# Low parts of the weights in the heads' stages: ScalarE's negative and an accumulating transfer in place of VectorE's subtraction

## The chip, the cores and the metric

One Trainium2 chip; the kernel runs on one of its cores. The metric is the device time of one execution in microseconds (us), the median of the runs shown. The engines are TensorE (PE), VectorE (DVE), ScalarE (ACT), GpSimd (POOL) and SyncE (SP), which only issues transfers here. HBM is the memory off the core; tiles live on the core in SBUF, and matmuls end in PSUM.

## The reference, cut to what matters

Two layers over 256 latent tokens, with 256 context tokens ahead of them in the attention and in the scan; the width is 1024, everything is float32.

```python
def layer(x, c):                             # adaLN: shift, scale, gate from c
    h = modulate(rmsnorm(x), shift, scale)
    p = h @ w_in                             # q, k, v, gMLP u and v, HGRN2 gates/q/v, merge gates
    y_att = diff_attention(q, k, v, lam)     # 8 heads: softmax(q1 k1) - lam softmax(q2 k2), times v
    y_gm  = spatial_gating(u, v)             # layernorm(v), a matmul over chunks of 128 tokens, times u
    y_hg  = both_directions(hgrn2_scan)      # 8 heads, keys of 128, values of 128, decays from log f
    y = sig(g0) * (y_att @ wa) + sig(g1) * (y_gm @ wg) + sig(g2) * (y_hg @ wh)
    x = x + gate * rmsnorm(y @ w_out)
    return x + gate2 * conv_ffn(modulate(rmsnorm(x), shift2, scale2))
```

Each weight is used in one projection and is read from HBM as the stage that needs it comes up.

## The kernel before, in words

TensorE multiplies in a form of float32 that keeps fewer bits of an operand (F32R). So each operand is held as two parts, a high part that is the rounded value, and a low part that is what the rounding left, and a product is three matmuls: high by low, high by high, low by high (`mm3`, L120 to L123; its matmuls are the lines L121 to L123).

The parts of a weight are made by `load_part` (L105 to L113), one chunk at a time. A chunk is 128x1024 float32, 512 KB. SP loads it into a tile `wr` (three buffers, L110); ACT casts it to `wh` (four buffers, L111); DVE subtracts, `wl = wr - wh` (four buffers, L112). A tile `wr` is free when cast and subtraction have read it; a `wh` or `wl` when the last matmul has read it.

A layer has a stage of heads (loop at L989 to L1002). In it the matmuls of two things alternate on PE, woven by `weave` (L819): on one side the projections of the next head, which use the weights (`project(h + 1)`: names in_w_hff, in_w_hqg, in_w_aqk, in_w_hi, in_w_av), and on the other side the two halves of head `h`, `hg_head` (the scan, with tiles E, K, w, sqs, sc; L505, L319, L541, L544) and `att_head` (the attention, with tiles p, s, wt; L600 scores, L617 transposes, L624 values). The work of those two between their matmuls is done by DVE, ACT and POOL. Beside the last head stands `tail_proj` (L647) in place of a projection: the weight in_w_gv in two halves of four chunks each, so that one half fills all four buffers of `wl`, and then the first part of in_w_gu in two chunks. PE's order of instructions is fixed by the code as it is written; the order on DVE, ACT and POOL is chosen by the scheduler, which places the loading, cast and subtraction of a weight as early as buffers allow. Each engine works its instructions in order, so that one which waits holds what is behind it.

Layer 0's stage of heads lies at 107 to 648 us of the profiled execution, its `tail_proj` from 562 us on; layer 1's at 1455 to 1862 us, its `tail_proj` from 1800 us on. In each of these stretches lie 64 chunks that the change touches: 42 of in_w_hff, in_w_hqg and in_w_aqk, 12 of in_w_hi and in_w_av, 8 of in_w_gv, 2 of in_w_gu.

Of the kernel before, what the change touches and what calls it, by code (L numbers as in the profile page):

```python
# [10 lines left out]
F32 = mybir.dt.float32  # L11
# [36 lines left out]
def trunk(ctx: ExitStack, tc: tile.TileContext, A, out):  # L48
    nc = tc.nc
    sub, mul, add, amin, amax = ALU.subtract, ALU.mult, ALU.add, ALU.min, ALU.max  # L50
# [9 lines left out]
    @contextmanager  # L60
    def pool(name, side="left", **tags):
        with tc.tile_pool(name=name, bufs=1, side=side, reuse_waits="tile") as p:
            def get(tag, shape, dt=F32):
                return p.tile(shape, dt, tag=tag, name=tag, bufs=tags[tag])
            yield get
# [36 lines left out]
        return pack[l][:, a:b]  # L102


    def load_part(src, k0, k1, eng):  # L105
        w = src.shape[-1]
        raw = wp.tile([P, 1024 // w, w], F32, tag="wr", name="wr", bufs=3)[:, :k1 - k0, :]
        hi = wp.tile([P, 1024 // w, w], F32R, tag="wh", name="wh", bufs=4)[:, :k1 - k0, :]
        lo = wp.tile([P, 1024 // w, w], F32R, tag="wl", name="wl", bufs=4)[:, :k1 - k0, :]
        nc.sync.dma_start(out=raw, in_=src[:, k0:k1, :])  # L110
        nc.scalar.copy(out=hi, in_=raw)  # L111
        eng.tensor_tensor(out=lo, in0=raw, in1=hi.bitcast(F32), op=sub)  # L112
        return [(hi[:, i, :], lo[:, i, :]) for i in range(k1 - k0)]  # L113

    def load_w(src, kt=8, early=True, engs=(nc.vector, nc.vector)):
# [249 lines left out]
    def hg_proj(get, l, h, X, NQ, out, pss=None):  # L365
        ls = get("lk", [P, 2, NT])
        k = get("lk", [P, 2, NT])
        qg = get("qg", [P, 2, NQ])

        def gate(d, ps):  # L370
            t = softplus_neg_abs(get, ps, NT)
            nc.vector.scalar_tensor_tensor(out=k[:, d, :], in0=ps, scalar=0.0, in1=t, op0=amax, op1=add)
            nc.vector.scalar_tensor_tensor(out=ls[:, d, :], in0=ps, scalar=0.0, in1=t, op0=amin, op1=sub)

        if pss is None:
            w = load_w(A["w_hff"][l, h])
            for d in range(2):
                ps = PB([P, 512])
                yield from fm_steps(w, d, X, NT, ps)
                gate(d, ps)  # L380
            w = load_w(A["w_hqg"][l, h])
            for j in range(2):
                ps = PB([P, 512])
                yield from fm_steps(w, j, X, NQ, ps)
                silu_of(get, qg[:, j, :], ps[:, :NQ], NQ)
        else:
            e = get("E", [P, 2, NQ])
            nc.scalar.copy(out=e[:, 0, :], in_=pss[0][:, :NQ])
            nc.vector.tensor_copy(out=e[:, 1, :], in_=pss[1][:, :NQ])
            for d in range(2):  # L390
                gate(d, pss[2 + d])
            for j in range(2):
                silu_of(get, qg[:, j, :], e[:, j, :], NQ)
        out.update(ls=ls, k=k, qg=qg)

    def v_proj(get, src, X, out, name, w=None):
        if w is None:
            w = load_w(src)
        v = get("v", [P, 4, 256])
        for tt in range(2):  # L400
            ps = PB([P, 2, 256])
            yield from tm_steps(w, X, (2 * tt, 2 * tt + 1), ps)
            nc.scalar.copy(out=v[:, 2 * tt:2 * tt + 2, :], in_=ps)
        out[name] = v
# [414 lines left out]
    def weave(main, n, sides, counts, rate):  # L819

        todo = sorted((((i + 1) / (c + 1) * n * rate, k) for k, c in enumerate(counts) for i in range(c)))
        done = 0
        end = object()
        while True:
            while todo and (todo[0][0] <= done or main is None):
                next(sides[todo.pop(0)[1]], None)
            if main is None:
                break
            if next(main, end) is end:
                main = None  # L830
            done += 1
        for g in sides:
            for _ in g:
                pass
# [4 lines left out]
    with pool("x0", side="right", x=4, n=4, h=4, wa=3, wb=3, scr=1, cr=1, wj=1) as get, \  # L839
# [65 lines left out]
        for i in range(KT + 1):  # L905
# [8 lines left out]
            if i:  # L914
                k = i - 1
                for g, ps in enumerate(first):
                    c = slice((g % 2) * P, (g % 2 + 1) * P)
                    hi, lo = w[g // 2][k]
# [16 lines left out]
    for l in range(DEPTH):  # L935
# [5 lines left out]
        def putter(b, h):  # L941
            return lambda t: nc.sync.dma_start(out=ysp[b, h], in_=t)
# [23 lines left out]
        with pool("heads", lk=2, qg=1, qk=1, v=3, w=2, sq=2, sqs=2 if l else 1, wt=2, sc=1, E=6 if l else 4, K=2, p=2) as get, ExitStack() as even, \  # L966
                tc.issue_after(pre.ins):
            gete = even.enter_context(pool("even", lk=2, qg=1, qk=1, t=3, sh=2))
            gets = [lambda tag, *a: (gete if tag in ("lk", "qg", "qk", "t", "sh") else get)(tag, *a),
                    lambda tag, *a: (gete if tag in ("t", "sh") else get)(tag, *a)]  # L970

            def project(h, out, pss=None):
                if pss is not None:
                    yield from hg_proj(gets[h % 2], l, h, Xh, NQ, out, pss)
                if h % 2 == 0:
                    yield from v_proj(get, A["w_hi"][l, h // 2], Xh, out, "vh", whi if h == 0 else None)
                if pss is None:
                    yield from hg_proj(gets[h % 2], l, h, Xh, NQ, out)
                yield from att_proj(gets[h % 2], l, h, Xh, rope, NQ, out)
                if h % 2 == 0:  # L980
                    yield from v_proj(get, A["w_av"][l, h // 2], Xh, out, "va")

            def units(h):
                return (12 if l == 0 else 9) + (8 if h % 2 == 0 else 0)

            d = {}
            for _ in project(0, d, first):
                pass
            for h in range(HEADS):  # L989
                j = slice((h % 2) * P, (h % 2 + 1) * P)  # L990
                m = [hg_head(get, l, h, d["ls"], d["k"], d["qg"][:, 0, :], d["qg"][:, 1, :], d["vh"][:, :, j], putter(1, h),
                             lbv, (reset, masks), NQ),
                     att_head(get, l, d["qk"], d["va"][:, :, j], putter(0, h), attv[l], NQ)]
                if h + 1 < HEADS:
                    main, n = project(h + 1, d), units(h + 1)
                else:
                    even.close()
                    getv = rvt.enter_context(pool("vt", side="right", vt=ns))
                    vt = [getv("vt", [P, D]) for _ in range(ns)]
                    pus = []  # L1000
                    main, n = tail_proj(l, Xh, vt, ns, NQ, pus), 8 * ns // 2 + ns
                weave(main, n, m, (13, 2 * ns + 3), 0.92 if h + 1 < HEADS else (0.7, 0.85)[l])  # L1002
        if l == 0:
            jobs += [(lambda get, scr, m=m: ada_row(get, scr, 0, m, 2)) for m in range(16, 48)]
        pre = nc.scalar.preload_act_table(AF.Gelu_apprx_tanh)
# [204 lines left out]
```

## Time and profile before

| | |
|---|---|
| median of 3 runs | 2241.21 us (2240.69 to 2246.49) |
| profiled execution, its own time | 2245.93 us |
| span of the profile | 2244.2 us |
| PE busy | 2128.5 us, 95% of the span |
| DVE busy | 1727.2 us, 77% |
| ACT busy | 1155.8 us, 52% |
| POOL busy | 324.7 us, 14% |
| queue of SP's transfers | 93042 packets, 290.59 MB |

The busy time of an engine is the time in which it had an instruction at work. An instruction's idle time is the time for which its engine stood still just before it, and the releaser is the work whose end let it go on. The granted clock of TensorE is given as a share of its full speed of 2.4 GHz. A transfer's landing is counted from its issue.

### The profile page before, as it was taken

To read this page: it belongs to the slowest core of one execution; us is meant where nothing else is said; L and a number is where in the kernel's file an instruction comes from. 1 tells how busy PE (TensorE), PEld (TensorE's weight loads), DVE (VectorE), ACT (ScalarE), POOL (GpSimd) and SP (SyncE) were. 2 spreads that over 40 slices of the span, in tenths; PEclk is the share of its full clock that TensorE was granted. 3 is DMA by queue.
4 is the path that set the end of the run, shared out by engine and by line. 5 is a ranking of instruction groups with operands and counts; after the bars stand their busy time and mean duration, and the time that the engine had idled before them with its cause. 6 is when DMAs were issued, how large, how long until landed. Compare 5 with 4: busy or idle time off the path is not lost. (4 is left out here: it accounts for less than half of the span.)

```text
span 2244.2 us, 32759 instructions
## 1 busy us (share of the span) xinstructions
PE 2128.5 (95%) x12400; PEld 1849.0 (82%) x12400; DVE 1727.2 (77%) x2885; ACT 1155.8 (52%) x1913; POOL 324.7 (14%) x276
## 2 busy tenths in 40 slices
PE   6999999999999999998999998999999989997998
PEld 4878888788888877877887877988888879997997
DVE  7799897998857884448876776898998976567786
ACT  3666565665553222335442333666666655456664
POOL 4332132321300000002000001222221210001000
PEclk9999999999999999999999999999999999999999
DMA  7222222122245665344555653222232336554554
GB/s 257 101 71 71 76 76 66 66 71 71 66 149 185 224 201 94 100 141 154 161 179 184 195 144 127 99 91 89 84 96 81 98 98 211 196 192 141 185 195 138
DMA packets 93488, 293.21 MB, mean 131 GB/s; under 512 B 16017, under 2 KB 20753, under 8 KB 93073
## 3 DMA queue, kind: packets, MB, share of 16 engines
q1 hardware_dynamic: 93042, 290.59, 39.9%
q8 instruction: 98, 1.61, 0.3%
q14 instruction: 60, 0.49, 0.1%
q10 hardware_dynamic: 288, 0.52, 0.1%
HBM read 282.66 MB, written 8.41 MB: 130 GB/s over the span
## 5 line engine op out<-in xcount | busy, mean ns | idle before, releaser
L121 PE MATMUL pm<-X,wh 128*128 128x512 f32 (+1 forms) x2032 | 715.8, 352 | 18.2 <-POOL X L253 9.8
L123 PE MATMUL pm<-X,wl 128*128 128x512 f32 (+1 forms) x2032 | 699.0, 344 | 1.2 <-POOL wl L112 1.2
L122 PE MATMUL pm<-X,wh 128*128 128x512 f32 (+1 forms) x2032 | 698.8, 344 | 0.0
L112 DVE TENSOR_TENSOR wl<-wr,wh 128x1024 fp32r<-128x1024 f32 x398 | 492.9, 1243 | 192.6 <-ACT wh L111 187.8
L111 ACT CAST wh<-wr 128x1024 fp32r<-128x1024 f32 x408 | 422.2, 1039 | 313.0 <-PE pm L122 188.3
L121 PEld LDWEIGHTS pm<-X,wh 128*128 128x128 f32 x2032 | 386.5, 190 | 69.1 <-POOL X L253 11.9
L123 PEld LDWEIGHTS pm<-X,wl 128*128 128x128 f32 x2032 | 386.6, 190 | 49.8 <-POOL wl L112 2.7
L122 PEld LDWEIGHTS pm<-X,wh 128*128 128x128 f32 x2032 | 386.3, 190 | 42.1
L225 DVE SCALAR_TENSOR_TENSOR wj<-wa,scr 128x1024 f32<-128x1024 f32 x128 | 156.3, 1221 | 63.8 <-DMA wa<-in_ada_row 60.9
L445 POOL TENSOR_TENSOR K<-qg,E 128x512 f32<-128x512 f32 (+1 forms) x96 | 130.6, 1362 | 466.6 <-PE ps L505 313.6
L121 PE MATMUL pm<-wl,X 128*128 128x256 f32 (+1 forms) x608 | 187.3, 308 | 0.0
L123 PE MATMUL pm<-wh,X 128*128 128x256 f32 (+1 forms) x608 | 183.4, 302 | 0.0
L122 PE MATMUL pm<-wh,X 128*128 128x256 f32 (+1 forms) x608 | 183.2, 301 | 0.0
L202 POOL TENSOR_TENSOR s<-s,mhalf 128x1 f32<-128x1 f32 x26 | 14.4, 552 | 1077.1 <-DVE s L199 1037.1
L121 PE MATMUL pm<-ys,wh 128*128 128x512 f32 (+1 forms) x384 | 129.8, 338 | 8.8 <-ACT wh L111 5.1
L439 DVE TENSOR_TENSOR E<-lk 128x512 f32<-128x512 f32 (+1 forms) x192 | 124.3, 680 | 9.5 <-PE ps L544 8.2
L123 PE MATMUL pm<-ys,wl 128*128 128x512 f32 (+1 forms) x384 | 129.6, 338 | 0.0
L122 PE MATMUL pm<-ys,wh 128*128 128x512 f32 (+1 forms) x384 | 129.4, 337 | 0.0
L121 PEld LDWEIGHTS pm<-wl,X 128*128 128x128 f32 x608 | 117.0, 192 | 6.4 <-issue 2.2
L122 PEld LDWEIGHTS pm<-wh,X 128*128 128x128 f32 x608 | 116.8, 192 | 4.2
L123 PEld LDWEIGHTS pm<-wh,X 128*128 128x128 f32 x608 | 116.6, 192 | 4.3
L440 ACT ACTIVATE E<-E 128x1024 f32<-128x1024 f32 (+1 forms) x96 | 80.8, 846 | 62.7 <-DVE E L439 61.5
(247 smaller groups left out, 3551.8 us busy)
## 6 DMA issues: line engine op xcount, KB each, us to landing
wr<-in_w_up SPq DMA_DIRECT2D x88, 512.0 KB, 4.3
wa<-in_ada_row SPq DMA_DIRECT2D x80, 512.0 KB, 4.1
wr<-in_w_gate SPq DMA_DIRECT2D x48, 512.0 KB, 4.2
wr<-in_w_dn SPq DMA_DIRECT2D x40, 512.0 KB, 4.2
wr<-in_w_hqg SPq DMA_DIRECT2D x32, 512.0 KB, 3.7
wr<-in_w_hff SPq DMA_DIRECT2D x32, 512.0 KB, 3.6
wr<-in_w_aqk SPq DMA_DIRECT2D x32, 512.0 KB, 3.6
wr<-in_w_hi SPq DMA_DIRECT2D x16, 512.0 KB, 4.2
```

The costliest lines, as they stand in the source:

```text
L111: nc.scalar.copy(out=hi, in_=raw)
L112: eng.tensor_tensor(out=lo, in0=raw, in1=hi.bitcast(F32), op=sub)
L121: nc.tensor.matmul(ps, lhsT=lh, rhs=rl, start=first, stop=False)
L122: nc.tensor.matmul(ps, lhsT=lh, rhs=rh, start=False, stop=False)
L123: nc.tensor.matmul(ps, lhsT=ll, rhs=rh, start=False, stop=last)
L202: nc.gpsimd.tensor_tensor(out=r, in0=r, in1=mhalf, op=ALU.pow)
L225: nc.vector.scalar_tensor_tensor(out=junk, in0=raw, scalar=1.0, in1=scr[:, v, :], op0=mul, op1=mul, accum_out=mod[l][:, m, v:v + 1])
L439: nc.vector.tensor_tensor(out=dst, in0=ref if first else src, in1=src if first else ref, op=sub)
L440: nc.scalar.activation(out=E, in_=E, func=AF.Exp)
L445: nc.gpsimd.tensor_tensor(out=mkap(KQ[:], dims, NQ), in0=mkap(q, dims), in1=mkap(E[:], [[2 * b, np_], [b - NQ, 2], [1, b]], NQ), op=mul)
```

## The change

A flag `lean` is set from behind `project(0)` to the end of the loop over the heads, in both layers. While it is set, DVE makes no low part. ACT writes the negative of the high part into `wl`, and a transfer that POOL issues reads the same chunk from HBM once more and adds it to what stands in `wl`. The sum is again `wr - wh`. Outside the flag nothing changes.

```diff
+    lean = [False]
+
     def load_part(src, k0, k1, eng):
...
         nc.sync.dma_start(out=raw, in_=src[:, k0:k1, :])
         nc.scalar.copy(out=hi, in_=raw)
-        eng.tensor_tensor(out=lo, in0=raw, in1=hi.bitcast(F32), op=sub)
+        if lean[0]:
+            nc.scalar.mul(out=lo, in_=hi.bitcast(F32), mul=-1.0)
+            nc.gpsimd.dma_start(out=lo, in_=src[:, k0:k1, :], accum_op=add)
+        else:
+            eng.tensor_tensor(out=lo, in0=raw, in1=hi.bitcast(F32), op=sub)
...
             for _ in project(0, d, first):
                 pass
+            lean[0] = True
             for h in range(HEADS):
...
                 weave(main, n, m, (13, 2 * ns + 3), 0.92 if h + 1 < HEADS else (0.7, 0.85)[l])
+        lean[0] = False
```

Over the whole program DVE has 128 subtractions fewer, ACT 128 instructions more, POOL issues 128 transfers, and 67 MB more are read. PE's order is the same. In the rows below the lines of the changed kernel stand 2 higher up to the cast (L113), and 6 higher behind `load_part` (L612 is L606 of before); L115 is ACT's negative, L116 the accumulating transfer.

The first place is DVE in layer 0, behind the attention's reciprocal of an odd head, where the trace of before has its clearest gap. Before (`wl` is the low part, `sc` the scores of the scan, K and E its keys and exponentials, p and s2 the attention's weights and their scales):

```order
L112 TENSOR_TENSOR wl_2613<-wr_2611,wh_2612 128x1024
L608 RECIPROCAL s2_2299<-s2_2299 128x2
L463 COPY_PREDICATED sc_2253<-masks_541,ps_2343 128x2x2x128
L609 TENSOR_TENSOR s2_2299<-s2_2299,attv_574 128x1
L443 TENSOR_TENSOR K_2372<-lk_1652,E_2368 128x512
L610 TENSOR_SCALAR p_2297<-p_2297,s2_2299 128x512
L439 TENSOR_TENSOR E_2534<-lk_1651 128x256x2
L611 SCALAR_TENSOR_TENSOR p_2297<-p_2297,s2_2299 128x512
L112 TENSOR_TENSOR wl_2619<-wr_2617,wh_2618 128x1024
L463 COPY_PREDICATED sc_2253<-masks_541,ps_2383 128x2x2x128
```

With the change the same place reads as follows (p_2315 and sc_2271 are p_2297 and sc_2253 of before):

```order
L469 COPY_PREDICATED sc_2271<-masks_541,ps_2361 128x2x2x128
L449 TENSOR_TENSOR K_2390<-lk_1660,E_2386 128x512
L445 TENSOR_TENSOR E_2554<-lk_1659 128x256x2
L614 RECIPROCAL s2_2317<-s2_2317 128x2
L445 TENSOR_TENSOR E_2554<-lk_1659 128x256x2
L615 TENSOR_TENSOR s2_2317<-s2_2317,attv_574 128x1
L428 SCALAR_TENSOR_TENSOR lk_2232<-reset_539,lk_2232 128x512
L616 TENSOR_SCALAR p_2315<-p_2315,s2_2317 128x512
L477 COPY s8_2564<-E_2561 128x4
L469 COPY_PREDICATED sc_2271<-masks_541,ps_2401 128x2x2x128
```

The two subtractions between the two copies into `sc` are gone; an instruction for E, the scan and a small copy stand there now.

The second place is ACT beside the last head of layer 0, in `tail_proj`: the casts of the second half of in_w_gv. Before (`vt` takes the projection's result, p and wt are the attention's):

```order
L606 ACTIVATE p,s_5499<-ps,s_5498 128x256 x2
L653 COPY vt<-pm 128x512
L619 COPY wt<-ps 128x512
L111 CAST wh<-wr 128x1024 x4
L653 COPY vt<-pm 128x512
L606 ACTIVATE p,s_5587<-ps,s_5586 128x256 x2
```

With the change:

```order
L612 ACTIVATE p,s_5557<-ps,s_5556 128x256 x2
L659 COPY vt<-pm 128x512
L625 COPY wt<-ps 128x512
L113 CAST wh<-wr 128x1024
L115 ACTIVATE wl<-wh 128x1024
L113 CAST wh<-wr 128x1024
L115 ACTIVATE wl<-wh 128x1024
L113 CAST wh<-wr 128x1024
L612 ACTIVATE p,s_5645<-ps,s_5644 128x256
L115 ACTIVATE wl<-wh 128x1024
L113 CAST wh<-wr 128x1024
L612 ACTIVATE p,s_5645<-ps,s_5644 128x256
```

A negative now stands behind each cast, so that each later cast comes one instruction later, and the attention's exponentials lie among them.

The third place is POOL over the same stretch, at the end of layer 0's stage of heads. Before (sh and qk are the attention's rotated projections, w, E and K the scan's):

```order
L577 TENSOR_TENSOR sh<-sh,sin 128x256
L583 TENSOR_TENSOR qk<-t,qk 128x256
L427 TENSOR_TENSOR w<-w,qg 128x512
L458 TENSOR_TENSOR E<-E,qg 128x512
L577 TENSOR_TENSOR sh<-sh,sin 128x256
L583 TENSOR_TENSOR qk<-t,qk 128x256
L445 TENSOR_TENSOR K<-qg,E 128x512 x4
```

With the change:

```order
L433 TENSOR_TENSOR w<-w,qg 128x512
L116 DMA wl<-in_w_gv 128x1024
L583 TENSOR_TENSOR sh<-sh,sin 128x256
L116 DMA wl<-in_w_gv 128x1024
L589 TENSOR_TENSOR qk<-t,qk 128x256
L451 TENSOR_TENSOR K<-qg,E 128x512 x3
L116 DMA wl<-in_w_gv 128x1024
L451 TENSOR_TENSOR K<-qg,E 128x512
L116 DMA wl<-in_w_gv 128x1024 x3
L116 DMA wl<-in_w_gu 128x1024 x2
```

The issues of the transfers stand between POOL's own multiplications, in POOL's one order: an issue waits for ACT's negative, and what is behind it waits with it.

## Rows read from the trace of the kernel before

**Rows 1.** Windows: start:end length; busy PE, PEld, DVE, ACT, POOL; PE clock, DMA share, GB/s.

```profile
107.00:562.00 455.00, 437.26 (x2574) 373.34 (x2572) 399.50 (x690) 281.70 (x495) 125.03 (x78) 0.99 0.21 71
562.00:648.00 86.00, 84.62 (x436) 70.55 (x437) 53.93 (x94) 41.90 (x72) 19.90 (x11) 1.00 0.22 71
1455.00:1800.00 345.00, 330.94 (x2221) 293.43 (x2220) 312.48 (x623) 228.54 (x441) 72.32 (x78) 1.00 0.27 88
1800.00:1862.00 62.00, 53.22 (x298) 44.99 (x297) 44.85 (x86) 35.35 (x62) 9.44 (x10) 0.92 0.36 115
```

**Rows 2.** Lines of PE, 107 to 648 us: busy, mean ns, idle before, releasers.

```profile
L505 PE MATMUL ps<-K 128*128 128x128 f32 x384 | 51.7, 277 | 2.7 <-DVE K L443 2.7
L624 PE MATMUL ps<-wt,v 128*128 128x128 f32 x192 | 27.2, 278 | 5.6 <-DVE sc L463 4.6 <-ACT wt L619 1.0
...
L319 PE MATMUL ps<-sqs,onesr 128*128 128x512 f32 x64 | 22.6, 435 | 6.7 <-DVE sqs L193 6.7
L617 PE MATMUL ps<-ident,p 128*128 128x128 f32 x96 | 16.6, 284 | 2.8 <-ACT p L606 2.8
```

**Rows 3.** Lines of PE, 1455 to 1862 us.

```profile
L600 PE MATMUL ps<-qk 64*128 64x512 f32 x96 | 15.8, 427 | 2.6 <-POOL qk L583 2.6
L319 PE MATMUL ps<-sqs,onesr 128*128 128x256 f32 x64 | 15.3, 322 | 10.3 <-DVE sqs L193 10.1
L617 PE MATMUL ps<-ident,p 128*128 128x128 f32 x64 | 10.3, 285 | 6.4 <-DVE p L611 4.2 <-DVE s L604 2.2
```

**Rows 4.** Timeline of DVE and PE around 260 us: start, length, idle before and releaser.

```profile
254.88 2.26 DVE L112 TENSOR_TENSOR wl<-wr,wh 128x1024 fp32r<-128x1024 f32 x1
...
262.13 1.21 DVE L112 TENSOR_TENSOR wl<-wr,wh 128x1024 fp32r<-128x1024 f32 x1
263.26 0.71 DVE L463 COPY_PREDICATED sc<-masks,ps 128x512 f32<-128x512 uint8 x1
...
264.03 1.16 PE L624 MATMUL ps<-wt,v 128*128 128x128 f32 x8 [1.51 <-DVE sc L463]
```

**Rows 5.** Lines of DVE, the subtraction, first 107 to 648 us, then 1455 to 1862 us.

```profile
L112 DVE TENSOR_TENSOR wl<-wr,wh 128x1024 fp32r<-128x1024 f32 x65 | 85.4, 1319 | 25.0 <-ACT wh L111 24.5
...
L112 DVE TENSOR_TENSOR wl<-wr,wh 128x1024 fp32r<-128x1024 f32 x67 | 86.6, 1298 | 9.9 <-ACT wh L111 9.3
```

**Rows 6.** Timeline: casts of the tails' tightest chunks, and the matmuls that first need them.

```profile
572.25 1.05 ACT L111 CAST wh<-wr 128x1024 fp32r<-128x1024 f32 x1 [0.33 <-PE pm L122]
...
576.89 0.39 PE L121 MATMUL pm<-wl,X 128*128 128x512 f32 x1
...
599.87 1.05 ACT L111 CAST wh<-wr 128x1024 fp32r<-128x1024 f32 x1 [1.24 <-PE pm L123]
...
606.23 0.48 PE L121 MATMUL pm<-wl,X 128*128 128x512 f32 x1
...
632.81 1.05 ACT L111 CAST wh<-wr 128x1024 fp32r<-128x1024 f32 x1 [0.77 <-PE pm L123]
...
637.15 0.39 PE L123 MATMUL pm<-X,wl 128*128 128x512 f32 x1
...
1806.12 1.03 ACT L111 CAST wh<-wr 128x1024 fp32r<-128x1024 f32 x1
...
1810.95 0.39 PE L121 MATMUL pm<-wl,X 128*128 128x512 f32 x1
```

**Rows 7.** Transfers: queue's packets, MB, share of 16 engines; issues with KB, us to landing.

```profile
q1 hardware_dynamic: 93042, 290.59, 39.9%
...
wr<-in_w_gv SPq DMA_DIRECT2D x16, 512.0 KB, 3.8
...
x<-xs SPq DMA_DIRECT2D x2, 512.0 KB, 8.6
```

**Rows 8.** Timeline of POOL beside the last head of layer 0.

```profile
566.83 6.33 POOL L583 TENSOR_TENSOR qk<-t,qk 128x256 fp32r<-128x256 f32 x1 [1.24 <-ACT qk L582]
...
578.33 0.72 POOL L583 TENSOR_TENSOR qk<-t,qk 128x256 fp32r<-128x256 f32 x1 [0.98 <-ACT qk L582]
```

## The prediction, made before the changed kernel had run

> **What bounds the kernel now.** I read the windows of the two stages of heads first, then PE's lines with what released them, then the timeline of one gap, and last the casts at the stages' ends. In the windows [rows 1] the reader is to see two things. PE is busy for 437.26 + 84.62 + 330.94 + 53.22 = 906.0 of 948 us, so it stands still for 42.0 us, and its granted clock is under full speed in two of the stretches: (1 - 0.99) x 455 = 4.6 us and (1 - 0.92) x 62 = 5.0 us of work are lost there. So no change to these stages that leaves PE's work as it is can bring much over 42 + 9.6, some 52 us. And DVE is the fullest engine beside PE: 399.50 of 455 us (88%) in layer 0, 312.48 of 345 (91%) in layer 1, while ACT has 62% and 66%.
>
> PE's lines name who is late. In layer 0 [rows 2] DVE's work ends waits of 2.7 (K) + 4.6 (sc) + 6.7 (sqs) = 14.0 us, ACT's 2.8 + 1.0. In layer 1 [rows 3] it is DVE again with 10.1 (sqs) + 4.2 + 2.2 = 16.5 us; POOL has 2.6. Together 30.5 of the 42 us are waits for DVE. The timeline [rows 4] shows one such wait: two subtractions, 2.26 and 1.21 us, stand on DVE between 254.88 and 263.34; right behind the second comes the copy into `sc` (263.26), and PE waits 1.51 us for it before the matmuls at 264.03. None of the two subtractions is wanted soon. So the subtractions do delay work on which PE waits.
>
> **What is removed.** 64 subtractions in each layer's stage. By their rows [rows 5] 64 x 1.319 = 84 us of DVE go in layer 0 and 64 x 1.298 = 83 us in layer 1. DVE's share falls from (399.50 + 53.93)/541 = 84% to 68%, and from (312.48 + 44.85)/407 = 88% to 67%. In the order of DVE at the place of rows 4 both subtractions are gone, and what moves up is work of the heads, little of it ahead of `sc`. In layer 0 I take the whole 14.0 us as saved, and 3 of the 4.6 us of clock, since the clock is low only where PE has stood still: 17 us. In layer 1 I take half, 8 of 16.5 us and 2.5 of 5.0: there the wait for `sqs` is a chain that goes from DVE to POOL, ACT, and DVE again, so a free DVE shortens only its own links. That is 10.5 us. The upper bound is all of DVE's waits and half of the clock, 30.5 + 5 = 36 us.
>
> **What is added on ACT.** 128 negatives of 128x1024. The trace has none; the nearest row is the cast of the same size on the same engine, 1.05 us [rows 6]. So 67 us are added in each layer: ACT goes from (281.70 + 41.90)/541 = 60% to 72% in layer 0, from (228.54 + 35.35)/407 = 65% to 81% in layer 1. Each stands behind its cast and holds what is behind both for 1.05 us more: the attention's exponentials p and the copy wt. Waits for ACT are 3.8 us in layer 0 [rows 2]. I let them double, and take 4 us off; the bound below is nothing, if the negatives fill idle time alone. What remains is a gain of 17 + 10.5 - 4 = 23 us.
>
> **What is added on POOL and in the queues.** 128 issues, and 512 KB read again by each. POOL is busy 145 of 541 and 82 of 407 us [rows 1], so it has room; its work in order is what counts (below). The second reads are 67 MB over 948 us, 71 GB/s beside the 71 to 115 that flow now, at a DMA share of 0.21 to 0.36: bandwidth is no bound.
>
> **What the accumulating transfer costs.** Before, the low part was there one subtraction after the cast. Now it takes a negative, POOL's issue, and a transfer that begins only when the negative has ended. I call X the time from the end of the negative to the landing. For most chunks X is covered: buffers fill early, and the first use comes 8 to 25 us after the cast's end. It is not covered where `tail_proj` fills all four buffers at once. There the cast waits for the buffer, and the distances from its end to the first use are [rows 6]: 576.89 - 573.30 = 3.6, 606.23 - 600.92 = 5.3, 637.15 - 633.86 = 3.3, and in layer 1 1810.95 - 1807.15 = 3.8 us. Each makes PE wait for 1.05 + X less the distance.
>
> No accumulating transfer and none of POOL's is in this trace, so X is bounded by neighbours. Below: the plain load of this size lands 3.8 us after SP's issue [rows 7], and nothing is taken for POOL or the adding. Above: the slowest transfer of this size takes 8.6 us [rows 7], and a second read (93042 packets take 39.9% of 16 engines' 2244 us, so 0.154 us each; 128 packets on 16 engines, 1.2 us) makes 9.8. I take 6: the plain 3.8, 1.2 for a source and a destination that must both be read, and 1 for POOL to come to the issue. It lies at the low side, since nothing in the stage has DMA queues full. With X = 6 the four waits are 3.45 + 1.75 + 3.75 + 3.25 = 12.2 us, and the second chunks of a half, whose casts now come a negative later, bring it to 13. I shifted all 128 chunks by the same rule: the waits are 5 us in all with X = 3.8, 19 with 7, 25 with 8, 35 with 9, 48 with 10, 78 with 12.
>
> The Trainium skill has a price ("DMA: Bandwidth & Descriptors", section "Anatomy of one DMA — SWDGE (gpsimd) path"): about 2.0 us and the bytes at 436 GB/s, an estimate of 3.2 us for such a transfer. It says nothing of the adding; by it X would be near 4 with a little for POOL, and the time near 2223. No row here shows a transfer of POOL's.
>
> **The sum.** 23 gained and 13 lost are 10 us. The profiled execution took 2245.93 us, so by its own time the changed kernel comes to 2236; the median of before lies 4.7 us lower, 2241.2, and against it the forecast is **2231 us**. A difference under 0.3% (6.7 us) counts as the same.
>
> **The rivals.**
>
> *The accumulating transfer lands late* (chance 0.25, slower). POOL must come to the issue, and make it, while DVE runs beside it. What speaks for it: a multiplication of 128x256 took POOL 6.33 us at 566.83 and 0.72 us at 578.33 [rows 8], and over that first one lay DVE's two-input work, so POOL can be held. It decides from where the waits eat the gain of 23, X = 7.7. With X = 9 the time is 2241 - 23 + 35 = 2253, with 10 2266, with 12 2296. Against it: DVE gets 84 us lighter here, and of its long streams the subtractions are the part that goes. A rule of the Trainium skill stands behind it ("SBUF — State Buffer", section "Who interferes with whom"): VectorE's work with two inputs shares a read interface with GpSimd, and transfers that GpSimd issues can be starved while VectorE holds the pair, though the page infers that two-input work does not stop the writing of descriptors. By its first half the 6.33 us are explained; by its last the issues are not held, and X stays at 6.
>
> *ACT takes DVE's place* (chance 0.2, the same). At 81% in layer 1 ACT is nearly as full as DVE was, and the chains that PE waits for go through ACT too. Then layer 1 gives nothing, and the waits at the tails stay: 2241 - 17 + 13 = 2237. Against it: ACT's own waits are long ones for other engines, so it has slack to give.
>
> *POOL's order holds its own products* (chance 0.05, slower). An issue that waits for the negative keeps the K and qk behind it waiting. PE now waits 2.6 us for qk in layer 1 [rows 3]. If each of the 28 writes of qk (two for each of seven heads in each layer) came 1 us later with no cover, 28 us would be lost: 2241 - 23 + 13 + 28 = 2259. Against it: POOL is busy for a quarter of the time, and the scheduler places issues behind the negatives.
>
> *The change does as said and X is small*: the forecast's own low side. With X = 3.8 and all of the 36 us the time is 2241 - 36 + 5 = 2210.
>
> **How the numbers follow.** The forecast has 0.5. Its own range is 2210 (above) to 2234, where it meets the band of no change. The late transfer reaches to 2266 with X = 9.8, the bound from the slowest row; beyond lie perhaps 0.1, and under 2208 less than 0.1. So the range is 2208 to 2266. Faster 0.5; the same 0.2, the ACT case; slower 0.3, the other two.
>
> **What would show it.** Right: DVE's share near 68% and PE's waits for sc, K, sqs and p gone in layer 0; four waits of PE for a transfer at L121 or L123, between 575 and 640 and near 1811, of 2 to 4 us each. The landing times of the transfers into `wl` give X itself. Wrong: waits for `wl` in the middle of heads, which need X over 8; PE's lines L617 and L624 released by ACT for more than 8 us; POOL's K or qk as releaser of more than 10 us. If the gaps for DVE are still there with the subtractions gone, the step from its share to PE's waits has failed. The prediction is wrong at large if the new waits cost the granted clock as well, as in layer 1's tail, where it is 0.92 now [rows 1].

## The result, and the profile after

The changed kernel takes 2298.3 us (2293.4 to 2302.99, 4 runs) against 2240.95 us: ratio 1.0255, 95% interval 1.0236 to 1.0275. It is slower by 57 us where 10 us of gain were forecast, and lies above the range, which ends at 2266. The profiled execution took 2296.19 us.

The windows of its two stages of heads, cut near the same matmuls (they lie at 107, 556 and 657 us and at 1455, 1783 and 1871 us of before; columns as in [rows 1]):

```profile
107.00:565.00 458.00, 431.94 (x2545) 367.49 (x2544) 339.90 (x627) 325.69 (x541) 144.31 (x132) 0.99 0.58 132
565.00:691.00 126.00, 106.65 (x503) 85.56 (x502) 53.97 (x105) 60.74 (x98) 20.16 (x20) 0.95 0.41 106
1485.00:1818.00 333.00, 315.92 (x2089) 278.80 (x2088) 247.23 (x538) 258.77 (x460) 108.47 (x126) 0.99 0.73 167
1818.00:1920.00 102.00, 83.89 (x503) 71.31 (x502) 60.99 (x122) 64.85 (x113) 21.91 (x26) 0.92 0.64 162
```

DVE has become light, as was meant: (339.90 + 53.97)/584 = 67% in layer 0, where it had 84%. PE has not become busier: it stands still for 26.1 us in the heads of layer 0 (17.4 between the same matmuls before) and 19.4 beside its last head (1.7), 17.1 (14.1) and 18.1 (8.8) in layer 1. The DMA share of the heads rose from 0.21 to 0.58 and from 0.27 to 0.73, while the bytes did not even double (71 to 132 and 88 to 167 GB/s).

PE's lines, first those of the weights over the whole span, then three of the heads from 107 to 565 us:

```profile
L129 PE MATMUL pm<-X,wl 128*128 128x512 f32 (+1 forms) x2032 | 701.4, 345 | 13.8 <-DMA wl<-in_w_gu 7.4 <-DMA wl<-in_w_hff 4.1 <-POOL wl L118 1.2
...
L127 PE MATMUL pm<-wl,X 128*128 128x256 f32 (+1 forms) x608 | 190.8, 314 | 24.2 <-DMA wl<-in_w_gv 21.1 <-DMA wl<-in_w_av 2.9
...
L511 PE MATMUL ps<-K 128*128 128x128 f32 x336 | 45.5, 278 | 1.2 <-DVE sc L469 1.2
...
L325 PE MATMUL ps<-sqs,onesr 128*128 128x512 f32 x52 | 17.6, 419 | 5.9 <-DVE sqs L199 5.6
L623 PE MATMUL ps<-ident,p 128*128 128x128 f32 x84 | 14.4, 280 | 13.2 <-DVE p L617 4.9 <-DVE sc L469 4.5 <-ACT p L612 3.7
```

Two things are to be seen. PE waits 7.4 + 4.1 + 21.1 + 2.9 = 35.5 us for accumulating transfers, 7 of them in the heads and the rest in the two tails. And in the heads, against [rows 2], the waits at the matmuls of K and of wt went from 2.7 + 5.6 to 1.2 us, but those at the transposes of p rose from 2.8 to 13.2 us: the gaps for DVE have moved to another line.

PE's order is the same in both kernels, and both traces have 12400 matmuls, so the n-th of each is the same work. Matched so, PE is 9 us late at the end of the heads of layer 0 (555.0 before, 564.1 after), 34.5 us at the end of that stage (657.4, 691.9), 30 us at the start of layer 1's heads (1455.0, 1484.7), 35 us before its tail (1783.0, 1818.2) and 49 us behind it (1871.9, 1921.3). The two tails lose 25 and 14 us, and the heads in front of them, which were to gain, lose 9 and 5.5.

One wait for each of the two weights in the tail of layer 0, in the timeline:

```profile
583.34 1.05 ACT L115 ACTIVATE wl<-wh 128x1024 fp32r<-128x1024 f32 x1
584.69 0.88 POOL L116 DMA_DIRECT2D wl<-in_w_gv  x1 [1.48 <-ACT qk L585]
592.57 0.68 PE L127 MATMUL pm<-wl,X 128*128 128x512 f32 x1 [4.96 <-DMA wl<-in_w_gv]
...
659.18 1.06 ACT L115 ACTIVATE wl<-wh 128x1024 fp32r<-128x1024 f32 x1
660.54 0.86 POOL L116 DMA_DIRECT2D wl<-in_w_gu  x1 [33.74 <-ACT wl L115]
668.74 0.79 PE L129 MATMUL pm<-X,wl 128*128 128x512 f32 x1 [6.14 <-DMA wl<-in_w_gu]
```

The negative ends at 584.39, POOL issues 0.30 us later, and the matmul goes on when the transfer lands, 8.2 us after the negative; the second time it is 8.5 us. Worked out in this way from the records of all 128 transfers, the wait for POOL is 0.30 us and X, from the end of the negative to the landing, is 7.8 us (medians), with X from 5.6 to 11.9; the last four chunks of in_w_gv, which follow each other within 7 us, have 8.8, 10.6, 11.7 and 11.9. The transfers' rows (columns as in [rows 7]):

```profile
q1 hardware_dynamic: 93042, 290.59, 38.9%
q0 software_dynamic: 18432, 67.12, 17.0%
...
wl<-in_w_gv POOLq DMA_DIRECT2D x16, 512.0 KB, 8.4
...
wl<-in_w_gu POOLq DMA_DIRECT2D x4, 512.0 KB, 8.8
```

A packet of POOL's queue takes 0.170 x 2294.4 x 16/18432 = 0.339 us of a DMA engine on average, one of SP's 0.154 us as before. Both averages hold packets of 4 bytes too (2048 of the 18432, 15857 of the 93042). By the trace's packet records a packet of 4096 bytes takes 0.377 us where it adds and 0.199 us in SP's queue.

### The profile page after: what moved, and what is told of

It is laid out like the page before. It is cut to its first block, busy times and chain, and to the rows that moved or that the text cites. A ratio compares the mean times of both kernels' runs of the same rounds, so it can differ in the third digit from the quotient of the medians.

```text
span 2294.4 us, 33018 instructions
## 1 busy us (share of the span) xinstructions
PE 2143.0 (93%) x12400; PEld 1853.9 (81%) x12400; DVE 1600.3 (70%) x2757; ACT 1271.1 (55%) x2041; POOL 393.2 (17%) x404
## 3 DMA queue, kind: packets, MB, share of 16 engines
q1 hardware_dynamic: 93042, 290.59, 38.9%
q0 software_dynamic: 18432, 67.12, 17.0%
## 5 line engine op out<-in xcount | busy, mean ns | idle before, releaser
L113 ACT CAST wh<-wr 128x1024 fp32r<-128x1024 f32 x408 | 422.0, 1038 | 305.8 <-PE pm L128 177.1
L118 DVE TENSOR_TENSOR wl<-wr,wh 128x1024 fp32r<-128x1024 f32 (+1 forms) x270 | 325.0, 1209 | 189.5 <-ACT wh L113 184.6
L127 PE MATMUL pm<-wl,X 128*128 128x256 f32 (+1 forms) x608 | 190.8, 314 | 24.2 <-DMA wl<-in_w_gv 21.1
L451 POOL TENSOR_TENSOR K<-qg,E 128x512 f32<-128x512 f32 (+1 forms) x96 | 113.7, 1187 | 238.7 <-PE ps L511 178.1
L115 ACT ACTIVATE wl<-wh 128x1024 fp32r<-128x1024 f32 x128 | 134.7, 1055 | 1.2
```

The lines of the kernel that those rows point to most:

```text
L115: nc.scalar.mul(out=lo, in_=hi.bitcast(F32), mul=-1.0)
L127: nc.tensor.matmul(ps, lhsT=lh, rhs=rl, start=first, stop=False)
L451: nc.gpsimd.tensor_tensor(out=mkap(KQ[:], dims, NQ), in0=mkap(q, dims), in1=mkap(E[:], [[2 * b, np_], [b - NQ, 2], [1, b]], NQ), op=mul)
```

## The experiments

| kernel | median us | ratio to before, 95% interval |
|---|---|---|
| no_low: no low parts in the heads | 2229.18 | 0.9946 (0.9927 to 0.9965) |
| neg_only: negatives, no transfer | 2244.72 | 1.0016 (0.9994 to 1.0039) |
| plain: transfer without adding | 2273.19 | 1.0142 (1.0127 to 1.0157) |
| half: half of each chunk added | 2277.23 | 1.0161 (1.0122 to 1.0200) |
| no_tail: changed way, but not beside the last head | 2260.24 | 1.0081 (1.0064 to 1.0097) |
| tail_only: changed way beside the last head alone | 2287.08 | 1.0183 (1.0148 to 1.0218) |
| neg_and_sub: before, and the negatives | 2264.17 | 1.0089 (1.0057 to 1.0121) |
| prio_no_low: no_low, p and sc first | 2230.97 | 0.9944 (0.9924 to 0.9963) |
| prio_before: before, p and sc first | 2238.37 | 0.9975 (0.9960 to 0.9990) |
| k_dve_no_low: no_low, K on DVE | 2200.71 | 0.9823 (0.9776 to 0.9870) |
| k_dve_before: before, K on DVE | 2229.16 | 0.9940 (0.9921 to 0.9958) |
| k_dve_after: the changed kernel, K on DVE | 2257.23 | 1.0074 (1.0047 to 1.0101) |
| k_dve_no_tail: no_tail, K on DVE | 2224.15 | 0.9926 (0.9903 to 0.9948) |
| k_dve_prio: prio_before, K on DVE | 2230.05 | 0.9947 (0.9929 to 0.9965) |
| pool_free: before, POOL's products in the heads on DVE | 2201.47 | 0.9833 (0.9796 to 0.9869) |
| pool_free_no_low | 2188.61 | 0.9768 (0.9741 to 0.9794) |
| pool_free_no_tail | 2211.79 | 0.9879 (0.9848 to 0.9911) |
| pool_dummy: pool_free, and idle products on POOL | 2236.96 | 0.9970 (0.9956 to 0.9983) |

### The change taken apart: no_low, neg_only, plain

```diff
 no_low:    -  nc.scalar.mul(...); nc.gpsimd.dma_start(...)
            +  return [(hi[:, i, :], hi[:, i, :]) for i in range(k1 - k0)]
 neg_only:  -  nc.gpsimd.dma_start(out=lo, in_=src[:, k0:k1, :], accum_op=add)
 plain:     -  nc.gpsimd.dma_start(out=lo, in_=src[:, k0:k1, :], accum_op=add)
            +  nc.gpsimd.dma_start(out=lo, in_=src[:, k0:k1, :])
```

> Leaves out the low parts of the heads' weights: nobody makes them, the high part is used in their place, so neither subtraction, negative nor transfer is left; the matmuls are as many as before. Theory T (the subtractions stood in DVE's way only in part; what moves up into their place are other instructions of the heads, and PE's waits in the middle of the heads stay): 2233 to 2241 us. Rival R1 (the subtractions did cost PE some 23 us, and something of the new way takes them back): 2215 to 2222 us, and the waits for sc, sqs and p between heads fall under half of 30 us.

> The negatives on ACT alone, no accumulating transfer (the low part is then only the negative of the high one). Theory T: 2236 to 2243 us, since without the transfers the waits at the ends of the stages (36 us) go and nothing else does. Rival R1 with the transfers as what takes the gain back: 2218 to 2225 us. Rival R2 (ACT takes it back): the same time as before here, and 2218 for the kernel with no low parts.

> The transfer from POOL's queue stays, at the same place and behind the same negative, but writes the weights instead of adding them (the low part is then the raw weight). Theory A (the adding is what is slow: an accumulating packet takes 0.34 us of a DMA engine where a plain one takes 0.15): end of negative to landing falls from 7.8 us at the median to 4.5 to 5.5, the DMA share in the heads of layer 0 from 0.58 to 0.40, the time to 2255 to 2268 us. Rival P (POOL's issue, or the write of descriptors beside DVE's work, is what is slow): landing as late as with the adding, 2290 to 2300 us.

The steps between them are the bill: taking the subtractions away gives 12 us (2241 to 2229), the negatives take 16 back (2245), a plain transfer behind each adds 28 (2273), and the adding another 25 (2298). no_low lies under the 2233 to 2241 of theory T and 7 us above R1's 2215 to 2222: of the 27.5 us that were counted for the relief, 12 are there. T's account, that PE's waits stay, holds for layer 0; all of the 12 us are in layer 1 (its stage runs from the same matmul to the same matmul in 405.6 us instead of 420.2; that of layer 0 in 556.1 instead of 553.5). In the heads of layer 0 (107 to 555 us) no_low's waits have moved to the transposes of p:

```profile
L510 PE MATMUL ps<-K 128*128 128x128 f32 x336 | 45.5, 278 | 1.7 <-DVE sc L468 1.7
...
L324 PE MATMUL ps<-sqs,onesr 128*128 128x512 f32 x52 | 18.4, 436 | 7.3 <-DVE sqs L198 7.0
L622 PE MATMUL ps<-ident,p 128*128 128x128 f32 x84 | 14.3, 279 | 7.5 <-DVE p L616 3.5 <-DVE sc L468 2.3 <-ACT p L611 1.7
```

neg_only lies 2 us over T's 2236 to 2243 and can't be told from the kernel before. T is not the reason, since no_low shows a gain that the negatives then take back: that is R2, with a gain of 12 us and not of 23. Between the same matmuls the negatives' 16 us lie in layer 1: its heads take 329.1 us instead of no_low's 320.7, its tail 88.6 instead of 81.6, and in layer 0 little changes.

plain lands sooner (X 5.5 us at the median) and takes less of the queue, so A's mechanism is there; the time is 5 us above A's range. P, that POOL is what is slow, falls: the wait for POOL is 0.30 us here too. Its rows:

```profile
q0 software_dynamic: 18432, 67.12, 9.8%
...
wl<-in_w_gv POOLq DMA_DIRECT2D x16, 512.0 KB, 6.3
```

### Half of each chunk: half

```diff
-  nc.gpsimd.dma_start(out=lo, in_=src[:, k0:k1, :], accum_op=add)
+  hk = (k1 - k0) // 2
+  nc.gpsimd.dma_start(out=lo[:, :hk, :], in_=src[:, k0:k0 + hk, :], accum_op=add)
```

> Each accumulating transfer adds half of its chunk only (256 KB of 512; the other half of the low part stays the negative of the high one). Theory A (what lands late is the transfer's own time on the DMA engines, which doubles by the adding and queues where four follow each other): end of negative to landing falls from 7.9 us in the mean to 5.5 to 6.3, the share of the queue from 17.0% to 8.5 to 9.5%, the time from 2298 to 2268 to 2282 us, like the plain transfer with its 2273. Rival F (a fixed price of each transfer of POOL's, whatever it moves): landing over 7 us, 2288 us or more.

```profile
q0 software_dynamic: 18432, 33.56, 9.1%
```

A holds: X falls to 5.5 us in the mean, the queue's share to 9.1%, the time by 21 us, to 4 us above plain. Half the bytes added cost about as much as all of them copied.

### Where it is lost: no_tail, tail_only

```diff
             for h in range(HEADS):
+                lean[0] = h + 1 < HEADS          # no_tail;  tail_only: h + 1 == HEADS
```

> The changed way in the projections beside heads 0 to 6 only; the weights beside the last head (10 of 64 chunks in each layer) go by DVE's subtraction again. Theory T with the waits at the ends of the stages as the loss: the 40 us that PE's matmuls fall back there go, 2252 to 2260 us, still above before by the first chunk's wait and the heads of layer 1. Rival M (the transfers in the middle of the heads do the harm and the end only shows it): over 2275 us.

> The changed way beside the last head alone: 10 chunks in each layer, 54 by DVE's subtraction. If the ends of the stages carry the loss and it adds up (2298 with both, 2260 without the ends): 2242 + 38 = 2280, from 2272 to 2286 us. Rival (the ends wait so long only since the transfers of the heads before have filled the queue): under 2262 us, with landings at the ends of under 8 us.

The losses are 18 and 43 us, 61 together against 57: they add up, and the 20 chunks of the tails carry 70% of them. tail_only came 1 us above the range given. Without the heads' transfers ahead of them the last four chunks of in_w_gv in layer 0 land 10.2 to 13.2 us after their negatives, so it is not a queue filled earlier: the four transfers of one half of the weight queue among themselves (10.2, 12.0, 13.2 and 13.2 us in the order of their issue), with plain loads of SP's beside them.

### ACT's negatives by themselves: neg_and_sub

```diff
-        else:
-            eng.tensor_tensor(out=lo, ...)
+            eng.tensor_tensor(out=lo, ...)       # behind nc.scalar.mul, no transfer
```

> DVE's subtractions as before, and ACT's negatives beside them (each low part is first written by ACT and then by DVE, so what is computed is the reference's). With no low parts the time was 2229, with the negatives alone 2245. Theory N1 (ACT's 67 us in each layer cost some 15 us by themselves, since the chains of the heads go through ACT): 2252 to 2262 us, with waits for p, w and wt released by ACT. Rival N2 (the negatives only take the place of a wait that DVE had made): 2240 to 2247 us.

Theory N1, with 20 us, a little over its range. PE's lines of the heads of layer 0:

```profile
L605 PE MATMUL ps<-qk 64*128 64x512 f32 (+1 forms) x168 | 24.1, 371 | 3.7 <-ACT p L611 3.7
...
L622 PE MATMUL ps<-ident,p 128*128 128x128 f32 x80 | 13.7, 284 | 9.8 <-ACT p L611 6.3 <-DVE p L616 3.5
```

ACT's p now ends waits of 10.0 us, where it ended 2.8 at L617 [rows 2]. An engine at 60% of a stage is not idle where the chain comes by: a cast and a negative are 2.1 us of ACT, and what stands behind them is late by as much. That is shown for layer 0 alone. In layer 1 the wait that grew is at the transposes as well, from 2.2 to 9.0 us, but DVE's s ends it. And the run holds a second change: each subtraction now waits for the negative too, so that DVE's idle time ahead of its subtractions goes from 13.7 to 22.5 us (107 to 555 us). What part of the 20 us comes in that way no run shows.

### Why a lighter DVE gives so little: the order, or POOL

In no_low there are no subtractions, and the same four heads still make PE wait in layer 0 (heads 0, 2, 4 and 6 by the loop's count; the odd ones if the first is counted as one). One of them (the first row is the same instruction while POOL is still):

```profile
268.08 0.47 DVE L616 SCALAR_TENSOR_TENSOR p<-p,s 128x256 f32<-128x256 f32 x1
...
278.83 3.50 POOL L450 TENSOR_TENSOR K<-qg,E 128x512 f32<-128x512 f32 x2 [5.08 <-ACT E L445]
279.72 1.49 DVE L616 SCALAR_TENSOR_TENSOR p<-p,s 128x256 f32<-128x256 f32 x1
281.35 0.41 PE L622 MATMUL ps<-ident,p 128*128 128x128 f32 x2 [1.14 <-DVE p L616]
```

p took 1.49 us beside POOL's K and 0.47 without, 1.02 us more, and PE waited 1.14 us for it: nearly the whole gap. The changed kernel has the same, at its clearest gap:

```profile
266.05 1.51 POOL L451 TENSOR_TENSOR K<-qg,E 128x512 f32<-128x512 f32 x1 [1.43 <-PE ps L511]
266.42 1.43 DVE L616 TENSOR_SCALAR p<-p,s 128x512 f32<-128x512 f32 x1
...
268.41 1.57 POOL L451 TENSOR_TENSOR K<-qg,E 128x512 f32<-128x512 f32 x1
268.49 2.06 DVE L617 SCALAR_TENSOR_TENSOR p<-p,s 128x512 f32<-128x512 f32 x1
...
272.57 0.66 PE L623 MATMUL ps<-ident,p 128*128 128x128 f32 x4 [1.35 <-DVE sc L469]
```

Two theories were tried: the scheduler's order (p and sc placed first) and POOL's product into K (made by DVE instead).

```diff
 prio_*:   +  with tc.high_priority():            # around the softmax of scores() and the copy into sc
 k_dve_*:  -  nc.gpsimd.tensor_tensor(out=mkap(KQ[:], dims, NQ), in0=mkap(q, dims),
           +  nc.vector.tensor_tensor(out=mkap(KQ[:], dims, NQ), in0=mkap(q, dims),
```

> No low parts, as in the run with 2229 us, and the attention's scale of p and the copy into sc placed first by the scheduler when they are ready. Theory O (with the subtractions gone PE still waits because the scheduler moves other work of the heads ahead of p and sc): the waits of 16.5 us in the heads of layer 0 fall under 10, the time to 2215 to 2223 us. Rival C (the chain of dependences sets them, whatever stands on DVE): 2226 to 2232 us, waits as before.

> The kernel before with the same priority for p and sc, and the subtractions kept. Theory O: the subtractions can be passed over as well, 2228 to 2237 us. Rival C: 2238 to 2246 us. A third way (what is passed over is late for PE in its turn, K or sqs): over 2246 us.

> No low parts, as in the run with 2229 us, and POOL's product into K is made by DVE, so that POOL seldom works beside DVE; DVE gets 96 products more (about 60 us over the program by DVE's own K at 0.4 to 0.7 us). Theory S (in layer 0 PE still waits for p because POOL's K and DVE's p hold each other: p took 1.49 us beside it, 0.47 alone): waits for p and sc in the heads of layer 0 fall from 7.5 + 1.7 to under 4, 2218 to 2226 us. Rival C (the chain of dependences sets them): 2227 to 2233 us. Rival D (DVE's longer list is late for K in its turn): over 2235 us, with waits for K.

> The kernel before, with its subtractions, and POOL's product into K on DVE; the result is the reference's. DVE goes from 84 to 88% to over 92% of the heads' stages. Theory S with a full DVE: 2238 to 2250 us, the gain at p given back at K and sqs. Rival D: over 2255 us.

The order is worth little: prio_no_low is no_low again, prio_before gains 6 us, at the edge of what was foreseen by rival C. Giving DVE more work, however, makes the kernel faster: by 28 us with no low parts, by 12 us with the subtractions kept. Both are more than any of the theories gave; S had the sign of the first alone. In k_dve_no_low the waits for p, sc and K in the heads of layer 0 are gone, and one line is left (107 to 555 us):

```profile
L324 PE MATMUL ps<-sqs,onesr 128*128 128x512 f32 x54 | 18.2, 419 | 8.2 <-DVE sqs L198 8.2
```

### The same in the changed kernel: k_dve_after, k_dve_no_tail, k_dve_prio

The edits are those above, together.

> The changed kernel with POOL's product into K on DVE, so that POOL's list in the heads is mostly the transfers. With no low parts this move was worth 28 us, with DVE's subtractions 13. Theory S (DVE's relief is eaten by DVE and POOL holding each other, in the changed kernel too): 2298 less 28, 2265 to 2275 us, with the waits for p in the heads of layer 0 (13.2 us) under half, and those for transfers as long as they were. Rival W (what PE no longer waits for DVE it waits for ACT's negatives and the transfers): 2280 us or more.

> The changed way beside heads 0 to 6 only, and POOL's product into K on DVE. From 2260 without the move. Theory S: 2230 to 2240 us, so that the change alone would be near no loss against the subtraction with the same move (2229). Rival W: 2245 us or more.

> The kernel before, with the product into K on DVE and the scheduler's priority for p and sc. If the two add up: 2229 - 6 = 2223 us. If the priority only helped where POOL held p: 2227 to 2231 us.

Theory S, and more of it than foreseen: 41 and 36 us. In the heads of layer 0 of k_dve_after PE waits 5.1 us in all, with all negatives and transfers at work there; the tails wait as before. Between the same matmuls these heads take 429.6 us, as in k_dve_no_low (430.0), so there the negatives' price, too, was one of POOL's. In layer 1 it was not: its heads take 326.1 us against 311.4 in k_dve_no_low, and 5.4 of PE's 10.8 us of waits there are for transfers. k_dve_no_tail (2224) and k_dve_before (2229) can't be told apart by their intervals: against the subtraction, the change outside the tails is then neither gain nor loss. The priority adds nothing to the move.

### All of POOL's products: pool_free, pool_free_no_low, pool_free_no_tail, pool_dummy

```diff
 pool_free:   w, K, E, sh and qk in the heads: nc.gpsimd.tensor_tensor -> nc.vector.tensor_tensor
 pool_dummy:  + nc.gpsimd.tensor_tensor(out=mkap(junk[:], dims), in0=mkap(q, dims),
              +                         in1=mkap(E[:], ...), op=mul)      # behind DVE's product into K
```

> The kernel before with all of POOL's products in the heads (w, K, E, sh, qk) on DVE: POOL has nothing left there. Theory S with room left: under 2229 us, waits for sqs, which come after POOL's w and E, fall from 6 to under 4 us in layer 0. Rival D (DVE, at 95% and more of the heads' stages, is the bound): 2235 us or more.

> No low parts, and none of POOL's products in the heads on POOL. It says what the subtractions cost where POOL and DVE no longer hold each other. PE's waits in the heads are 4.6 + 1.2 + 0.1 + 5.3 = 11 us with the subtractions kept and POOL free, at 2201 us. Theory S (the subtractions cost PE next to nothing once DVE runs at its own speed): 2192 to 2201 us. Rival E (DVE's fullness is a cost by itself): under 2190 us.

> POOL's products on DVE, and the changed way beside heads 0 to 6, so that POOL issues transfers alone. The result is the reference's. By theory S the negatives and transfers can then only cost: 2201 plus the waits for transfers in the heads (8 us with the product into K on DVE) and clock, 2206 to 2216 us. Rival E (DVE's fullness is a cost by itself): 2198 us or less.

> The kernel with POOL's products on DVE (2201 us), and beside it POOL makes each product for K once more, into a tile that nobody reads (as 16 bit numbers, for want of room). The result is the reference's; no chain of the heads goes through POOL. Theory H (a product on POOL and the work on DVE beside it hold each other): DVE's instructions get longer again, 2215 to 2235 us. Rival L (POOL's products only cost since they take longer than DVE's, 1.7 us against 0.68, in the chains that PE waits for): 2199 to 2206 us.

pool_free computes all that the reference does, and at 2201 us beats both kernels. Part 1 of its page (busy time by engine), and PE's waits in the heads of layer 0 (107 to 541 us):

```profile
PE 2115.8 (96%) x12400; PEld 1844.6 (84%) x12400; DVE 1728.7 (79%) x3077; ACT 1156.6 (53%) x1913; POOL 78.3 (4%) x84
```

```profile
L505 PE MATMUL ps<-K 128*128 128x128 f32 x336 | 45.2, 277 | 0.6 <-DVE K L445 0.6
...
L319 PE MATMUL ps<-sqs,onesr 128*128 128x512 f32 x52 | 17.3, 414 | 1.1 <-DVE sqs L193 1.1
...
L512 PE MATMUL ps<-E 128*128 128x128 f32 x28 | 5.8, 289 | 2.9 <-ACT wt L619 2.9
```

DVE makes 3077 - 2885 = 192 instructions more than before and is busy for 1728.7 us against 1727.2: POOL's 246 us cost DVE 1.5 us, since DVE's other instructions got shorter by nearly what the products take. In the heads of layer 0 a subtraction takes 1214 ns on average where it took 1308, the instruction for E at L439 682 ns where it took 815. Part 1 of pool_dummy's page, where 96 products stand on POOL again, outside of every chain:

```profile
PE 2123.2 (95%) x12400; PEld 1841.8 (83%) x12400; DVE 1777.7 (80%) x3077; ACT 1153.7 (52%) x1913; POOL 223.5 (10%) x180
```

DVE's 3077 instructions take 49 us longer, and the kernel 35 us (31 by the two ratios, since the kernel before was slower beside it). Rival L, by which POOL's products only cost as slow links of the chains, falls; theory H came out 2 us above its range.

pool_free_no_low says what the subtractions cost where nothing is on POOL: 13 us, as much as before (12), which is under S's range and in E's. But E's reason, that a full DVE is a cost by itself, is not shown, for the 13 us do not lie where DVE is full. Between the same matmuls the heads take 425.2 and 310.6 us against 427.8 and 309.7 in pool_free: there the subtractions cost some 2 us in all, as S has it, and 20 us with K alone moved (439.4 and 321.6 in k_dve_before, 430.0 and 311.4 in k_dve_no_low). The rest is 5 us in the tail of layer 1 and 6 us behind it, in code that is the same in both. pool_free_no_tail loses 10 us to pool_free, as theory S gave.

## Why the prediction was wrong, point by point

**What bounds the kernel.** Read rightly as far as it went: PE waits for DVE, and the gaps lie where the rows showed them. That the subtractions were the reason was a reading of one timeline [rows 4]. The same timeline holds what filled DVE:

```profile
249.49 0.49 DVE L610 TENSOR_SCALAR p<-p,s 128x512 f32<-128x512 f32 x1
...
253.72 2.34 POOL L445 TENSOR_TENSOR K<-qg,E 128x512 f32<-128x512 f32 x1 [20.49 <-PE ps L505]
...
257.82 1.80 POOL L445 TENSOR_TENSOR K<-qg,E 128x512 f32<-128x512 f32 x1 [1.76 <-PE ps L505]
258.40 1.50 DVE L610 TENSOR_SCALAR p<-p,s 128x512 f32<-128x512 f32 x1
```

Between the two subtractions, one instruction of DVE for p took 1.50 us, and 0.49 at 249.49 with POOL still; POOL's K was at work beside it from 257.82 to 259.62. The first subtraction, too, took its 2.26 us beside POOL's K, the second 1.21 without. The row of POOL at 6.33 us [rows 8] was taken as a sign for the transfers' issues, and it was a sign of the same thing seen from POOL's side.

**Step that failed first: the whole 14.0 us saved in layer 0, half in layer 1.** Measured with no low parts: nothing in layer 0, some 14 us in layer 1, 12 in all instead of 27.5. The step from DVE's share to PE's waits failed: in the heads of layer 0 PE stood still for 16.5 us instead of 17.4, and the waits went from the matmuls of K and of the values to the transposes of p. What held p there was POOL's product into K beside it: with that product on DVE as well (k_dve_no_low) the waits in these heads fall to 7.3 us, all for sqs.

**Second: ACT's negatives at 4 us.** The price of one was right (1.055 us on average, 1.05 taken). What they cost was 16 us in place of the subtractions and 20 beside them. So of the gain of 23 nothing was left before any transfer: neg_only is at 1.0016 of before (0.9994 to 1.0039). In layer 0 of neg_and_sub the added waits are for ACT's p; in the heads of layer 1 DVE ends most of them, and the way from the negatives to them stays open. The rival that had ACT take DVE's place was right in kind, and too small.

**Third: X = 6.** It was 7.8 at the median, and 8.8 to 11.9 in the eight chunks of the second halves of in_w_gv. POOL's part was guessed well: 0.30 us wait and 0.88 for the issue, against 1. The 1.2 us for reading a source and a destination was the term that was too small: adding took X from 5.5 (plain) to 7.8, 2.3 us. It had been worked out from 0.154 us a packet, an average with the short packets in it. An accumulating transfer takes 18432/128 x 0.339/16 = 3.05 us of all 16 engines, and four in a row queue, so that X is no single number. That the prediction's rule gives 35 us with X = 9, and 35.5 were measured, is luck as far as the number goes: with the median of 7.8 it gives some 24. The range's end of 2266 belongs to X = 10; with the 9.8 named beside it the rule gives some 3 us less. The sum left out the clock, which the last sentence of the prediction names: 0.95 and 0.92 in the tails where 1.00 and 0.94 stood between the same matmuls, (1 - 0.95) x 126 = 6.3 us in layer 0. There the clock fell to the lower of its two levels, 1.2 GHz, at 592.7, 626.9 and 667.8 us, behind or in PE's waits of 4.96, 4.35 and 6.14 us for transfers, and stood there for 13.6 us in all.

**The rivals.** The late transfer gave 2296 us with X = 12, and 2298 came: the right place, the weights of the tails, but with the wrong reason, and the number is luck. POOL was not held in its issues, X came near 12 for four chunks alone, and the gain of 23, which it kept, was not there. POOL's order as a rival (28 us) did not show: of the waits at the scores (L606), 1.6 us in the heads of layer 0, none is POOL's.

**What DVE and POOL do to each other, and the price of a transfer.** The rule of the Trainium skill on VectorE's two-input work and GpSimd ("SBUF — State Buffer", section "Who interferes with whom") agrees with the runs: 0.47 against 1.49 us for p, and 49 us over pool_dummy. It was weighed for the issues alone, where the page infers no harm and the 0.88 us agree; that it bears on POOL's products and DVE's work beside them was overlooked. The price of the skill ("DMA: Bandwidth & Descriptors", section "Anatomy of one DMA — SWDGE (gpsimd) path"), 3.2 us by estimate, does not hold here: without adding 4.8 to 7.6 us were measured from issue to landing by weight, with adding 6.4 to 8.8, and the measurement decides.

**What stays open.** How much of pool_dummy's 35 us is DVE's longer instructions and how much the longer hold on the tiles E that its products read; the hold shows little, for three waits of DVE, 1.9 us in all, end with such a product. Why the subtractions cost 6 us behind the stages in pool_free, where for some 130 us the matmuls follow each other 4% more slowly without a wait and at the full clock. And what the negatives cost by themselves with K on DVE: every run with that move and the negatives has the transfers too.

## What to carry to other kernels

When an engine is full and late, look at how long the same instruction takes there with and without its neighbour before taking work off it: here moving work onto the full engine gave 38 us, and the work that looked in the way cost 12. Price a transfer that replaces an instruction at its tightest users, where several follow each other, and with the engine time that the operation takes, not the bytes. An engine's share of a stage did not tell here whether it was free when the chain came by.

## What the runs showed of the hardware that was not expected

- By the packet records, a packet of 4096 bytes that adds took 0.377 us of a DMA engine (the changed kernel), a copied one from the same queue 0.214 us (plain), one of SP's queue 0.199 us. A packet of 2048 bytes with adding took 0.199 us (half), one of SP's queue 0.100 us.
- POOL's issue of a transfer took 0.88 us with adding and 0.58 without (plain), and DVE's work beside it hardly delayed it: 0.89 us on average for the 66 issues of the changed kernel that lay beside DVE's two-input work, 0.88 for the other 62.
- 192 products moved from POOL to DVE, 246 us of POOL's time, added 1.5 us to DVE's busy time.
